# A list scheduler with narrow matmuls kept together, a second modulation group on TensorE, and softmax scaling on GpSimd

## The chip, the cores and the metric

One Trainium2 chip; the kernel runs on one of its cores. The metric is device microseconds of the execution. The kernel before takes 1565.89 us, the median of three runs (1565.12 to 1569.17).

## What is computed

A network of three layers in fp32 on 256 tokens of width 1024. Layer 0 works on two streams, the tokens x and a context ctx of 256 rows; layer 1 uses the context for keys and values only; the second block has tokens alone. What the change touches is the modulation and the softmax of the first two layers:

```python
ml = (silu(c) @ w_mod[i] + b_mod[i]).reshape(B, 6, 1, D)      # i = 0, 1
mc = (silu(c_ctx) @ w_mod[i] + b_mod[i]).reshape(6, D)
hl = rms_norm(xl) * (1 + ml[:, 1]) + ml[:, 0]                 # and hc from mc
oc, ol = mla_pool_mixer(hc, hl, ...)  if i == 0  else  gqa_mixer(...)
xl = xl + ml[:, 2] * ol
xl = xl + ml[:, 5] * conv_ffn(rms_norm(xl) * (1 + ml[:, 4]) + ml[:, 3], ...)
# layer 0: the same for xc with mc
s = einsum('bqhgd,bkhd->bhgqk', q, k) * scale
p = softmax(s)                                                # 8 heads in either mixer
o = einsum('bhgqk,bkhd->bqhgd', p, v)
```

Layer 0's mixer is latent attention (8 heads, queries of x on 512 keys, queries of ctx on 256) beside a pooling branch (cumulated means over windows of 2, 4, 8 and 16); layer 1's is grouped-query attention on 512 keys. The second block has a swiglu FFN, differential and dilated attention, gates, and another swiglu FFN.

## The kernel before

**Products.** Every weight arrives as a piece of up to 1 MB in one of three `raw` buffers. ScalarE (ACT) copies it to fp32r, `whi`; VectorE (DVE) subtracts that from the piece and has the rest, `wlo`. Activations are split the same way, and `mm3` makes of each product three fp32r matmuls (hi hi, hi lo, lo hi), `mm2` two.

**Order.** Nothing is issued as it is written. `Program` records each operation with its engine, its dependences and a priority (its index in the program, with a shift that a few places set). `schedule` then simulates the engines: it gives each operation the duration that `price` returns, takes on each engine the ready operation that is first by priority, hands out the slots of the pools (34 activations, 3 raw, 7 tmp, 24 small, 8 PSUM banks and so on), and sorts by simulated start. What comes out is each engine's program, which the chip runs in that order, whatever the real durations are. So `price`, the latencies and the DMA rate decide only the order. Each recorded operation is issued from one line, L401 in the profile of before.

**Modulation.** `silu(c) @ w_mod` has only two rows (token and context), so it is not done as other products. Pieces 0 and 1 of layer 0, which the first norm needs, come in eight chunks (`mod_chunk`): 16 fp32 matmuls of 32 columns by 128 each, four column groups of the PE array side by side (`mod<-wm,sc`), then a matmul with `sel`. The other pieces are six groups, `MODS` (`mod_group`), in eight steps k:

- group 0 (piece 2, both streams; in `WHOLE`) is done on TensorE: at each k four narrow fp32 matmuls, one per column group, 512 columns each (`mod<-raw,sc`). They are recorded at the end of each head of layer 0's attention (`fill`).
- groups 1 to 5 are done on DVE: at each k the weights are multiplied by one number per partition and added to an accumulator `macc` of 128x1024, once for each stream (a TENSOR_SCALAR at k = 0, a SCALAR_TENSOR_TENSOR at the seven others); at the end, narrow matmuls with a column of ones sum over the partitions (`mod<-macc,one`). Group 1 (piece 4, both streams) is recorded beside the products `uk`, `uv` and `uq` of the attention's start (`early`); groups 2 to 5 beside layer 0's FFN.

**Start.** 100 matmuls of a constant tile (`warm`) are recorded in `setup` with a shift that lets real work pass them. While they run, the first chunks of modulation and weights arrive.

**Layer 0's mixer.** Products `cq`, `ckv` and `p` per stream; GpSimd (POOL) makes running sums of p (`pp`); the raw products are copied from PSUM (`cqraw`), transposed on TensorE (`cT`) and scaled; then the attention.

**Softmax** (`softmax_t`): DVE takes the row's negative maximum from PSUM, ACT makes the exponentials with their sum, DVE the reciprocal, and `times` scales the tile of exponentials `e`: in layer 0 on DVE for x (16 tiles of 128x512) and on ACT for ctx (16 of 128x256), in layer 1 on ACT (16 of 128x512). TensorE then transposes two scaled tiles into one bank (`pt`); the result is split and multiplied by v (`o`).

**FFN.** `modnorm` makes `h`, the normed and modulated input of layer 0's FFN, for both streams: a column sum, POOL's power -1/2, a spread over rows on TensorE (`rows`), and for each of 8 pieces two DVE and two ACT operations. `layer0_ffn` then starts the products `g` and `u`.

Of the kernel before, what the change touches and what calls it, by code (L numbers as in the profile page):

```python
# [29 lines left out]
WHOLE = (0,)  # L30
# [125 lines left out]
class Op:  # L156
    __slots__ = ("engine", "method", "args", "kw", "prio", "deps", "users", "n", "ready", "cost", "roots", "new",
                 "start", "end", "index", "outs")
# [10 lines left out]
class Program:  # L169
# [3 lines left out]
    TO_TENSOR = 110.0  # L173
    TABLES = {AF.Exp: 1, AF.Silu: 2, AF.Sin: 2, AF.Sigmoid: 3}
# [3 lines left out]
    DMA_RATE = 330.0  # L178
# [17 lines left out]
    def record(self, engine, method, args, kw):  # L196
        op = Op()
        op.engine, op.method, op.args, op.kw = engine, method, args, kw
        op.index = len(self.ops)
# [18 lines left out]
        for v in outs:  # L218
            g = self.region(v)
            r = v.root  # L220
            if r.cls == "psum" and engine == "tensor":
                if r.lastpe is not None:
                    op.deps.add(r.lastpe)
                r.lastpe = op.index
            for o, q in r.writes + r.reads:
                if o != op.index and self.overlap(g, q):
                    op.deps.add(o)
            cover = lambda q: g[0] <= q[0] and q[1] <= g[1] and g[2] <= q[2] and q[3] <= g[3] and \
# [16 lines left out]
    def price(op):  # L245
# [5 lines left out]
        if op.engine == "tensor":  # L251
            if m == "transpose":
                return 109.0 * n / 128
            width = out.parts[1] - out.parts[0]
            if op.kw["lhsT"].root.dtype == F32R:
                return n / 2.4 * (1 if n >= 256 else 4) + 2.5
            c = max(128, n) * 4 / 2.4 + 2.5
            return c * 0.25 + 15 if width == 32 else c
        if op.engine == "scalar":
            src = op.args[1]  # L260
            extra = sum(93 for k in ("scale", "bias") if isinstance(op.kw.get(k), View))
            return (0.833 * n + (52 if src.root.cls == "psum" else 93) + extra
                    + (60 if op.kw.get("accum_out") is not None else 0))
# [9 lines left out]
        if op.engine == "gpsimd":  # L273
            if op.kw.get("op") == ALU.pow:
                return 300 + 165.0 * n
            return 100 + n * {"tensor_tensor": 2.3, "tensor_scalar": 1.46, "memset": 0.8}.get(m, 3.5)
        return 60.0

# [4 lines left out]
    def schedule(self, capacity):  # L283
# [21 lines left out]
        dma, heat, table = 0.0, {}, None  # L305
# [6 lines left out]
        while len(order) < N:  # L312
            best = None
            for e in self.ENGINES:
                if avail[e]:
# [13 lines left out]
            _, i = heapq.heappop(avail[e])  # L329
# [17 lines left out]
            for r in need:  # L347
                free[r.cls].sort()
                r.slot = free[r.cls].pop(0)[1]
                live[r.cls][front:r.first] += 1  # L350
            op.start = t
            cost = op.cost
# [10 lines left out]
            if e == "sync":  # L363
                begin = max(t, dma)
                dma = begin + self.nbytes(op) / self.DMA_RATE
                op.end = dma + self.DMA_LATENCY
# [38 lines left out]
class Net:  # L405
# [159 lines left out]
    def setup(self):  # L565
# [19 lines left out]
        for _ in range(100):  # L585
            nc.tensor.matmul(ps[:, :T], lhsT=warm[:, :P], rhs=warm, start=True, stop=True)
# [41 lines left out]
    def mod_chunk(self, k):  # L628
        nc = self.nc
        ps = self.ps("mod")  # L630
        for i in range(KD // 2):
            for q in range(4):
# [3 lines left out]
                                 start=(i == 0), stop=(i == KD // 2 - 1))  # L636
        sb = self.tmp(P, "modsb")
# [5 lines left out]
    def mod_group(self, g):  # L643
# [6 lines left out]
        for k in range(KD):  # L650
            r = self.raw(f"wmod{g + 1}", k, 4 * w)
            if g in WHOLE:
                ps = ps or self.ps("mod")
                for q in range(4):
                    nc.tensor.matmul(ps[32 * q:32 * q + 32, :w], lhsT=self.sc[:, k, :], rhs=r[:, q * w:(q + 1) * w],
                                     start=(k == 0), stop=(k == KD - 1))
            else:
# [11 lines left out]
        ps = ps or self.ps("mod")  # L669
        for s in range(streams if acc else 0):  # L670
            for q in range(4):
                h, o = divmod(q * w, D)
                nc.tensor.matmul(ps[32 * q:32 * q + 32, :w], lhsT=self.one[:, s], rhs=acc[h, s][:, o:o + w],
                                 start=(s == 0), stop=(s == streams - 1))
        sb = self.tmp(w, "modsb")
# [56 lines left out]
    def times(self, engine, x, r):  # L732
# [3 lines left out]
        else:  # L736
            self.nc.vector.tensor_scalar(x, x, r, None, op0=ALU.mult)
# [40 lines left out]
    def layer0_mixer(self):  # L778
# [194 lines left out]
        for hd in range(8):  # L973
# [13 lines left out]
            for s in range(2):  # L987
                k0, nk = (0, 4) if s == 0 else (T, 2)
                es = []
                for j in range(2):  # L990
# [4 lines left out]
                    es.append(self.softmax_t(pscore[:, :nk * P], nk * P, "scalar" if s else "vector"))  # L995
# [66 lines left out]
    def layer0_ffn(self, acc):  # L1062
# [3 lines left out]
        acc2 = [self.acc(s) for s in range(2)]  # L1066
        fill = self.mod_groups(range(2, len(MODS)))
# [70 lines left out]
    def layer1(self, acc):  # L1138
# [27 lines left out]
        for b in range(4):  # L1166
# [13 lines left out]
            for hd in range(2):  # L1180
                kv = (b * 2 + hd) // 4
                es = []
                for j in range(2):
# [3 lines left out]
                    es.append(self.softmax_t(pscore, 512, "scalar"))  # L1187
# [695 lines left out]
```

## Time and profile before

| | before |
|---|---|
| median of three runs | 1565.89 us (1565.12 to 1569.17) |
| the profiled execution | 1562.85 us |
| its span, first to last instruction | 1561.1 us |
| mean granted TensorE clock | 0.997 |
| busy: PE, PEld, DVE, ACT, POOL | 98%, 86%, 74%, 53%, 6% |
| DMA | 258.47 MB, mean 166 GB/s |

The span is what the trace covers; the execution's time is 1.75 us longer. PE is the matmul engine and PEld its weight load, which runs beside it. A matmul's record can be longer than what it adds to the stream, because matmuls are pipelined; what one adds is read from the next one's start, or from the chain of waits. An fp32 matmul leaves two records, so four narrow matmuls are "x8" there.

### The profile page before, as it was taken

The page shows a single profiled execution, that of the slowest core. Times are in us where ns is not written, and L with a number is a line of the kernel's source. Part 1 is how long each engine was busy: PE and PEld are TensorE (multiplying, and loading weights), DVE is VectorE, ACT ScalarE, POOL GpSimd, SP SyncE. Part 2 cuts the span into 40 slices and gives each one's busy share as a digit, 9 for nine tenths or more (in the row PEclk, how much of TensorE's full clock was granted, in tenths as well). Part 3 has the DMA queues.
Part 4 walks back from the last instruction along what each step waited for, and adds up shares of the span by engine and source line. Part 5 has one row for each costly group of instructions (what it writes and reads, how often), then busy time and mean ns, then how long its engine had stood idle before and what let it go on. Part 6 is the DMA issues. An engine that isn't in the chain of part 4 may idle for free.

```text
span 1561.1 us, 23690 instructions
## 1 busy us (share of the span) xinstructions
PE 1534.3 (98%) x9226; PEld 1340.2 (86%) x9226; DVE 1147.6 (74%) x2117; ACT 829.1 (53%) x1532; POOL 100.1 (6%) x116
## 2 busy tenths in 40 slices
PE   9989999999999999999999999999999999999998
PEld 7877798888788888999888888888999999888886
DVE  5598889648964856889987787765887786687752
ACT  5356844231331334686876675554765565475550
POOL 0040000000000000110000011100000000111100
PEclk9999999999999999999999999999999999999999
DMA  9345353334753642222665564455423345454450
GB/s 373 117 133 215 135 177 133 123 109 180 257 185 133 245 155 86 84 107 109 237 221 192 177 227 162 163 206 197 166 87 114 122 168 200 173 216 162 162 189 27
DMA packets 41375, 258.47 MB, mean 166 GB/s; under 512 B 4784, under 2 KB 5168, under 8 KB 15664
## 3 DMA queue, kind: packets, MB, share of 16 engines
q1 hardware_dynamic: 41264, 256.97, 45.9%
q8 instruction: 72, 1.18, 0.3%
q14 instruction: 39, 0.32, 0.1%
HBM read 255.90 MB, written 1.05 MB: 165 GB/s over the span
## 4 chain that ended last, share of the span: by engine, by line
PE 88%; DVE 4%; ACT 1%; issue 1%; POOL 1%; DMA 0%; DVEq 0%; POOLq 0%; ACTq 0%; SPq 0%
PE g L401 18%; PE u L401 18%; PE dn L401 12%; PE tm L401 10%; PE y L401 8%; PE out L401 4%; PE gate L401 3%; PE s L401 3%; PE o L401 3%; PE pt L401 2%; PE pa L401 1%; PE mod L401 1%; PE uq L401 1%; DVE wlo L401 1%; DVE h L401 1%
## 5 line engine op out<-in xcount | busy, mean ns | idle before, releaser
L401 DVE TENSOR_TENSOR wlo<-raw,whi 128x1024 fp32r<-128x1024 f32 (+4 forms) x393 | 460.3, 1185 | 81.7 <-PE y L401 26.8
L401 ACT ACTIVATE whi<-raw 128x1024 fp32r<-128x1024 f32 (+4 forms) x393 | 394.1, 1025 | 221.5 <-PE dn L401 59.8
L401 PE MATMUL dn<-mid,whi 128*128 128x512 f32 (+1 forms) x576 | 172.2, 373 | 0.0
L401 PE MATMUL g<-h,whi 128*128 128x512 f32 (+1 forms) x528 | 169.7, 388 | 0.9 <-ACT h L401 0.8
L401 PE MATMUL u<-h,whi 128*128 128x512 f32 (+1 forms) x528 | 167.9, 385 | 0.0
L401 PE MATMUL tm<-whi,a 128*128 128x256 f32 (+1 forms) x576 | 126.8, 306 | 0.1
L401 PEld LDWEIGHTS dn<-mid,whi 128*128 128x128 f32 x576 | 105.0, 188 | 20.4 <-issue 0.8
L401 PE MATMUL dn<-mid,wlo 128*128 128x256 f32 (+1 forms) x376 | 121.6, 323 | 0.0
L401 PE MATMUL g<-a,whi 128*128 128x512 f32 x336 | 118.9, 392 | 0.0
L401 PE MATMUL u<-a,whi 128*128 128x512 f32 x336 | 118.7, 392 | 0.0
L401 PEld LDWEIGHTS g<-h,whi 128*128 128x128 f32 x528 | 99.2, 190 | 22.6 <-ACT h L401 0.9
L401 PEld LDWEIGHTS u<-h,whi 128*128 128x128 f32 x528 | 98.8, 188 | 19.8
L401 PE MATMUL g<-h,wlo 128*128 128x256 f32 (+1 forms) x344 | 115.0, 335 | 0.4 <-DVE wlo L401 0.4
L401 PE MATMUL u<-h,wlo 128*128 128x256 f32 (+1 forms) x344 | 114.6, 333 | 0.0
L401 PE MATMUL y<-whi,mid 128*128 128x512 f32 x352 | 109.0, 389 | 0.0
L401 DVE SCALAR_TENSOR_TENSOR macc<-raw,sc,macc 128x1024 f32<-128x1024 f32 x84 | 107.0, 1298 | 2.6 <-DMA raw<-wmod 2.4
L401 PEld LDWEIGHTS tm<-whi,a 128*128 128x128 f32 x576 | 95.2, 190 | 1.4 <-DVE a L401 0.3
L401 PE MATMUL g<-a,wlo 128*128 128x256 f32 x336 | 94.2, 280 | 0.0
L401 PE MATMUL u<-a,wlo 128*128 128x256 f32 x336 | 94.1, 280 | 0.0
L401 POOL TENSOR_TENSOR small<-small,mhalf 128x2 f32<-128x2 f32 (+2 forms) x34 | 34.2, 1007 | 895.1 <-DVE small L401 725.3
L401 PE MATMUL tm<-wlo,a 128*128 128x256 f32 (+1 forms) x288 | 87.6, 305 | 0.0
L401 PEld LDWEIGHTS y<-whi,mid 128*128 128x128 f32 x352 | 66.1, 188 | 13.7
(342 smaller groups left out, 3205.4 us busy)
## 6 DMA issues: line engine op xcount, KB each, us to landing
raw<-wup SPq DMA_DIRECT2D x44, 1024.0 KB, 4.8
raw<-wgu SPq DMA_DIRECT2D x44, 1024.0 KB, 4.8
raw<-wmod SPq DMA_DIRECT2D x32, 1024.0 KB, 5.0
raw<-wd SPq DMA_DIRECT2D x20, 1024.0 KB, 4.7
raw<-wdn SPq DMA_DIRECT2D x16, 1024.0 KB, 4.8
raw<-win2a SPq DMA_DIRECT2D x12, 1024.0 KB, 4.8
raw<-win2d SPq DMA_DIRECT2D x12, 768.0 KB, 4.2
wm<-wmod SPq DMA_DIRECT2D x16, 512.0 KB, 10.6
```

Source lines behind the costliest of these rows:

```text
L401: getattr(getattr(nc, op.engine), op.method)(*[res(a) for a in op.args], **{k: res(v) for k, v in op.kw.items()})
```

## The change

- `WHOLE` is now (0, 1): group 1 is done on TensorE as group 0 is, with four narrow matmuls of 256 columns at each k (32 in all). Its 16 `macc` operations and four of its narrow matmuls per stream are gone.
- `together` ties the narrow matmuls of one chunk, one k or one group: the first inherits the dependences of all, and `schedule` issues them back to back.
- Scheduler: a PSUM tile counts as one region in the dependences; entering and leaving narrow matmuls costs 90 and 230 ns in the model; a weight load sets a least distance of 109 ns between matmuls; DVE and POOL exclude each other in the model where `shared` says so; the DMA rate is 400 instead of 330, with a beginning of 2 us and at most 8 transfers ahead; other prices.
- 50 `warm` matmuls instead of 100.
- All 48 scalings of `e` in the two mixers go to POOL, as tensor_scalar.
- The first `macc` operation of group 2 waits in the model for the end of layer 0's `modnorm` (`late`).

The diff, cut to its core:

```diff
-WHOLE = (0,)
+WHOLE = (0, 1)
...
-    DMA_RATE = 330.0
+    DMA_RATE = 400.0
+    DMA_BEGIN = 2000.0
+
+    DMA_DEPTH = 8
...
+    def together(self, i):
+
+        group = self.ops[i:]
+        for op in group[1:]:
+            group[0].deps |= {d for d in op.deps if d < i}
+        for a, b in zip(group, group[1:]):
+            a.next = b
...
     def region(v):
+        if v.root.cls == "psum":
+            return (0, P, 0, v.root.ix.size)
...
+            if self.shared(op):
+                other = "gpsimd" if e == "vector" else "vector"
+                t = max(t, port[other])
+                port[e] = t + cost
+            if e == "tensor":
+                load = self.load(op)
+                t = max(t, begun + load)
+                if narrow != (load == 0.0):
+                    t = max(t, clock[e] + (self.LEAVE if narrow else self.ENTER))
+                begun, narrow = t, load == 0.0
+                follow = op.next
...
-        for _ in range(100):
+        for _ in range(50):
             nc.tensor.matmul(ps[:, :T], lhsT=warm[:, :P], rhs=warm, start=True, stop=True)
...
             if g in WHOLE:
                 ps = ps or self.ps("mod")
+                first = len(nc.ops)
                 for q in range(4):
                     nc.tensor.matmul(ps[32 * q:32 * q + 32, :w], lhsT=self.sc[:, k, :], rhs=r[:, q * w:(q + 1) * w],
                                      start=(k == 0), stop=(k == KD - 1))
+                nc.together(first)
...
                             nc.vector.tensor_scalar(acc[h, s], x, c, None, op0=ALU.mult)
+                            if g == 2:
+                                nc.ops[-1].deps.add(self.late)
...
-            self.nc.vector.tensor_scalar(x, x, r, None, op0=ALU.mult)
+            getattr(self.nc, engine).tensor_scalar(x, x, r, None, op0=ALU.mult)
...
-                    es.append(self.softmax_t(pscore[:, :nk * P], nk * P, "scalar" if s else "vector"))
+                    es.append(self.softmax_t(pscore[:, :nk * P], nk * P, "gpsimd"))
...
         acc2 = [self.acc(s) for s in range(2)]
+        self.late = len(self.nc.ops) - 1
         fill = self.mod_groups(range(2, len(MODS)))
...
-                    es.append(self.softmax_t(pscore, 512, "scalar"))
+                    es.append(self.softmax_t(pscore, 512, "gpsimd"))
```

What each engine issues: PE 8957 instructions before and 8931 now, DVE 2119 and 2087, ACT 1394 and 1362, POOL 121 and 169, the DMA queue 289 both times.

**Three places in the order.** In a row, a tile's name comes with its number in the program, and "x4" is four such instructions in a row. First, PE in layer 0's attention, before: `mod` are the narrow matmuls of group 0, `s` scores, `o` products with v, `pt` transposes of `e`.

```order
L401 MATMUL o_1733<-pT_1720,v_1236 64x256
L401 MATMUL mod_1533<-raw_1591,sc 32x512
L401 MATMUL s_1737<-qkT_1358,qkT_1639 128x512
...
L401 MATMUL pt_1832<-ident,e_1790 128x128
L401 MATMUL mod_1533<-raw_1591,sc 32x512
L401 MATMUL pt_1836<-ident,e_1790 128x128
L401 MATMUL mod_1533<-raw_1591,sc 32x512
L401 MATMUL s_1842<-qkT_1367,qkT_1692 128x256 x3
```

and with the change:

```order
L459 MATMUL s_1735<-qkT_1579,qkT_1572 128x512 x3
L459 MATMUL mod_1473<-raw_1519,sc 32x512 x4
L459 MATMUL o_1760<-pT_1723,v_1138 64x256 x3
...
L459 MATMUL s_2001<-qkT_1929,qkT_1924 128x256
L459 MATMUL mod_1473<-raw_1581,sc 32x512 x4
L459 MATMUL qkT_2039<-ident,qk_1132 96x128
```

Before, the 32 matmuls of group 0 stand at 15 places of PE's order; now they stand at 8, four at each. The chunks of `mod_chunk` (128 matmuls) stood at 15 places and stand at 8. The 32 new matmuls of group 1 stand at 8 places among `uk`, `uv` and `uq`.

Second, DVE at the copy of `cq` out of PSUM (`cqraw`), for which PE's transposes `cT` wait; `df` and `d` belong to the pooling branch. Before:

```order
L401 TENSOR_SCALAR macc_1054<-raw_785,sc 128x1024
L401 SCALAR_TENSOR_TENSOR df_1060<-pp_183_1025,pp_110 128x512
L401 TENSOR_TENSOR wlo_1067<-raw_594,whi_1040 128x1024
L401 TENSOR_TENSOR d_1072<-df_1060,d_1072 128x512
L401 TENSOR_SCALAR macc_1090<-raw_785,sc 128x1024
L401 SCALAR_TENSOR_TENSOR macc_1054<-raw_1019,sc,macc_1054 128x1024
L401 SCALAR_TENSOR_TENSOR macc_1090<-raw_1019,sc,macc_1090 128x1024
L401 COPY cqraw_1126<-cq_942 128x384
```

and with the change:

```order
L459 SCALAR_TENSOR_TENSOR df_963<-pp_179_932,pp_86 128x512
L459 TENSOR_TENSOR wlo_971<-raw_593,whi_944 128x1024
L459 TENSOR_TENSOR d_974<-df_963,d_974 128x512
L459 TENSOR_TENSOR wlo_1012<-raw_593,whi_995 128x1024
L459 TENSOR_TENSOR pp_183_1022<-pp_183_1022,consts 128x2
L459 COPY cqraw_1049<-cq_883 128x384
```

The four `macc` operations ahead of the copy are gone, and a second `wlo` stands there.

Third, DVE at the entry of layer 0's FFN, where POOL waits for `small` (the column sum of the second stream). Before:

```order
L401 SCALAR_TENSOR_TENSOR h_2963<-X_84,mods,rows_2903 128x256
L401 SCALAR_TENSOR_TENSOR h_2967<-X_84,mods,rows_2903 128x256
L401 TENSOR_SCALAR small_2973<-sum_2910 128x2
L401 SCALAR_TENSOR_TENSOR macc_2540<-raw_2877,sc,macc_2540 128x1024
L401 SCALAR_TENSOR_TENSOR h_2970<-h_2963,mods,h_2970 128x256
```

and with the change:

```order
L459 SCALAR_TENSOR_TENSOR h_2891<-X_84,mods,rows_2827 128x256
L459 TENSOR_SCALAR small_2898<-sum_2834 128x2
L459 RECIPROCAL sig<-lamL 128x1
L459 TENSOR_SCALAR ovs<-lamL 128x1
L459 TENSOR_TENSOR siglam<-sig,lam 128x1
L459 SCALAR_TENSOR_TENSOR h_2894<-h_2886,mods,h_2894 128x256
```

The `macc` of group 2 behind `small` is gone from here; its first one stands behind the last `h` of the second stream. Some operations of one column, for the second block, stand here instead.

## Rows read from the trace of the kernel before

**Rows 1.** The page: busy us and share of each engine; shares of the chain that ended last.

```profile
PE 1534.3 (98%) x9226; PEld 1340.2 (86%) x9226; DVE 1147.6 (74%) x2117; ACT 829.1 (53%) x1532; POOL 100.1 (6%) x116
...
PE 88%; DVE 4%; ACT 1%; issue 1%; POOL 1%; DMA 0%; DVEq 0%; POOLq 0%; ACTq 0%; SPq 0%
```

**Rows 2.** Windows: stretch, length, busy us (instructions) of engines, PEclk, DMA share, GB/s.

```profile
20.00:40.00 20.00, 19.46 (x200) 14.79 (x199) 13.40 (x29) 9.93 (x20) 0.71 (x1) 1.00 1.03 410
...
93.58:96.99 3.41, 3.24 (x13) 2.85 (x14) 3.34 (x17) 1.16 (x4) 2.39 (x3) 0.50 0.49 173
...
243.77:247.18 3.41, 3.41 (x18) 3.41 (x17) 3.41 (x11) 1.67 (x4) 0.00 (x0) 0.50 0.00 0
```

**Rows 3.** PE's waits over the span: us in total, times, longest us.

```profile
PE cT L401 <- DVE cqraw L401: 4.8, 1, 4.8
```

**Rows 4.** Timeline, 82 to 97 us (start us, us, engine, operation; idle before in brackets).

```profile
85.22 6.92 POOL L401 TENSOR_TENSOR pp<-pp 128x542 f32<-128x542 f32 x4 [1.29 <-DVE df L401]
...
89.12 4.11 DVE L401 SCALAR_TENSOR_TENSOR macc<-raw,sc,macc 128x1024 f32<-128x1024 f32 x2
93.15 0.55 DVE L401 COPY cqraw<-cq 128x384 f32<-128x384 f32 x1
...
93.75 1.33 PE L401 MATMUL cT<-ident,cqraw 128*128 128x128 f32 x5 [4.77 <-DVE cqraw L401]
```

**Rows 5.** The chain of waits, 120 to 180 us: start us, us, what.

```profile
125.00 0.62 PE mod L401 x8
...
128.12 1.06 PE mod L401 x8
...
133.50 0.99 PE mod L401 x8
...
142.58 0.97 PE mod L401 x2
...
178.32 0.98 PE mod L401 x4
```

**Rows 6.** By tile (macc, pp): count, duration ns min/median/max, first and last start, forms.

```profile
L401 DVE SCALAR_TENSOR_TENSOR macc<-raw,sc,macc x84: 1273/1278/2099, 89.1 to 551.1; 128x1024 f32<-128x1024 f32 x84
L401 DVE TENSOR_SCALAR macc<-raw,sc x12: 742/746/1580, 82.9 to 509.1; 128x1024 f32<-128x1024 f32 x12
L401 POOL TENSOR_TENSOR pp<-pp x10: 1091/1524/2118, 75.4 to 96.0; 128x542 f32<-128x542 f32 x4, 128x538 f32<-128x538 f32 x3, 128x530 f32<-128x530 f32 x2, 128x514 f32<-128x514 f32 x1
L401 POOL MEMSET pp<- x4: 547/552/699, 0.8 to 2.4; 128x544 f32 x4
```

**Rows 7.** Timeline of PE at the start.

```profile
17.16 3.28 PE L401 MATMUL warm<-warm 128*128 128x256 f32 x26
...
28.59 0.41 PE L401 MATMUL mod<-wm,sc 128*32 128x128 f32 x2
28.93 0.50 PE L401 MATMUL p<-h,wlo 128*128 128x512 f32 x1
```

**Rows 8.** Timeline at the entry of the first FFN.

```profile
247.10 1.27 DVE L401 SCALAR_TENSOR_TENSOR macc<-raw,sc,macc 128x1024 f32<-128x1024 f32 x1
...
247.26 1.67 POOL L401 TENSOR_TENSOR small<-small,mhalf 128x2 f32<-128x2 f32 x1 [6.55 <-DVE small L401]
...
248.99 0.71 PE L401 MATMUL rows<-ident,small 128*128 128x128 f32 x4 [0.64 <-POOL small L401]
```

**Rows 9.** POOL by tile small (columns as in Rows 6).

```profile
L401 POOL TENSOR_TENSOR small<-small,mhalf x34: 550/734/1674, 10.7 to 1555.8; 128x2 f32<-128x2 f32 x24, 128x1 f32<-128x1 f32 x6, 128x4 f32<-128x4 f32 x4
```

**Rows 10.** Groups by form: count, busy us, mean ns, idle before.

```profile
L401 DVE TENSOR_SCALAR e<-e,small 128x512 f32<-128x512 f32 x16 | 7.7, 479 | 0.2
L401 ACT ACTIVATE e<-e,small 128x512 f32<-128x512 f32 x16 | 10.8, 727 | 0.0
L401 DVE TENSOR_TENSOR wlo<-raw,whi 128x1024 fp32r<-128x1024 f32 x348 | 421.7, 1224 | 77.4 <-PE y L401 26.8 <-PE dn L401 18.2 <-ACT whi L401 12.9
```

**Rows 11.** Windows of the second layer's mixer (columns as in Rows 2).

```profile
sum 98.00, PE 97.11 PEld 92.09 DVE 84.88 ACT 70.79 POOL 13.70; mean PE 13.87 PEld 13.16 DVE 12.13 ACT 10.11 POOL 1.96
```

More of the change, by code (lines that the diff above doesn't have):

```diff
@@ L157 @@
     __slots__ = ("engine", "method", "args", "kw", "prio", "deps", "users", "n", "ready", "cost", "roots", "new",
-                 "start", "end", "index", "outs")
+                 "start", "end", "index", "outs", "next")
 class Engine:
@@ L198, in record @@
         op.engine, op.method, op.args, op.kw = engine, method, args, kw
+        op.next = None
         op.index = len(self.ops)
@@ L252, in price @@
             if m == "transpose":
-                return 109.0 * n / 128
-            width = out.parts[1] - out.parts[0]
+                return 55.0
             if op.kw["lhsT"].root.dtype == F32R:
-                return n / 2.4 * (1 if n >= 256 else 4) + 2.5
-            c = max(128, n) * 4 / 2.4 + 2.5
-            return c * 0.25 + 15 if width == 32 else c
+                return n / 2.4 + 13.3
+            return 0.4 * n if out.parts[1] - out.parts[0] == 32 else 222.0
         if op.engine == "scalar":
@@ L261, in price @@
             extra = sum(93 for k in ("scale", "bias") if isinstance(op.kw.get(k), View))
-            return (0.833 * n + (52 if src.root.cls == "psum" else 93) + extra
-                    + (60 if op.kw.get("accum_out") is not None else 0))
+            return (0.833 * n + (52 if src.root.cls == "psum" else 110) + extra
+                    + (92 if op.kw.get("accum_out") is not None else 0))
         if op.engine == "vector":
@@ L274, in price, with load, shared @@
             if op.kw.get("op") == ALU.pow:
-                return 300 + 165.0 * n
+                return 700.0
             return 100 + n * {"tensor_tensor": 2.3, "tensor_scalar": 1.46, "memset": 0.8}.get(m, 3.5)
         return 60.0
+    @staticmethod
+    def load(op):
+        if op.method != "transpose" and op.outs[0].parts[1] - op.outs[0].parts[0] == 32:
+            return 0.0
+        return 109.0
+    @staticmethod
+    def shared(op):
+        big = [v for v in list(op.args) + list(op.kw.values()) if isinstance(v, View)
+               and v.root.cls != "psum" and not any(v is o for o in op.outs)]
+        if op.engine == "gpsimd":
+            return len(big) > 0
+        if op.engine != "vector":
+            return False
+        big = [v for v in big if v.ix.size > 1]
+        return len(big) > 1 or (op.method in ("tensor_copy", "tensor_scalar") and len(big) == 1
+                                and op.outs[0].root.cls != "psum")
     def nbytes(self, op):
@@ L304, in schedule @@
         clock = {e: 0.0 for e in self.ENGINES}
-        dma, heat, table = 0.0, {}, None
+        dma, heat, table = self.DMA_BEGIN, {}, None
+        port = {"vector": 0.0, "gpsimd": 0.0}
+        begun, narrow, follow = 0.0, False, None
+        landed = []
         done = np.zeros(N + 1, bool)
@@ L314, in schedule @@
             for e in self.ENGINES:
-                if avail[e]:
+                if e == "tensor" and follow is not None:
+                    t = clock[e]
+                elif avail[e]:
                     t = clock[e]
@@ L328, in schedule @@
                 heapq.heappush(avail[e], (p, i))
-            _, i = heapq.heappop(avail[e])
+            if e == "tensor" and follow is not None:
+                i = follow.index
+                avail[e].remove((follow.prio, i))
+                heapq.heapify(avail[e])
+            else:
+                _, i = heapq.heappop(avail[e])
             op = ops[i]
@@ L350, in schedule @@
                 live[r.cls][front:r.first] += 1
+            cost = op.cost
+            if self.shared(op):
[9 more added lines that the diff above has]
+                follow = op.next
             op.start = t
[L352 removed]
             if e == "tensor":
@@ L363, in schedule @@
             if e == "sync":
+                landed.append(op)
+                if len(landed) > self.DMA_DEPTH:
+                    t = max(t, landed[-1 - self.DMA_DEPTH].end)
+                    op.start, clock[e] = t, t + cost
                 begin = max(t, dma)
@@ L653, in mod_group @@
                 ps = ps or self.ps("mod")
+                first = len(nc.ops)
                 for q in range(4):
@@ L656, in mod_group @@
                                      start=(k == 0), stop=(k == KD - 1))
+                nc.together(first)
             else:
@@ L669, in mod_group @@
         ps = ps or self.ps("mod")
+        first = len(nc.ops)
         for s in range(streams if acc else 0):
@@ L674, in mod_group @@
                                  start=(s == 0), stop=(s == streams - 1))
+        if acc:
+            nc.together(first)
         sb = self.tmp(w, "modsb")
```

3 lines of the change are left out of this document (2 added, 1 removed).

## The prediction

> **What bounds the kernel now.** I read the page first: PE is busy for 98% of the span and holds 88% of the chain that ended last [rows 1]. So the end moves only by what PE's own stream loses or gains; DVE, ACT and POOL count where PE waits for them. Next I looked for the places where PE issues less than it could: the windows, PE's list of waits, the timeline, the chain. They show four kinds. (a) PE stands once for 4.77 us, for the copy of `cq` out of PSUM [rows 3, 4]; right behind it the granted clock is 0.50, that is 1.2 instead of 2.4 GHz, from 93.58 to 96.99 us [rows 2]. A second stretch of that kind follows the waits at the FFN's entry, 243.77 to 247.18 us [rows 2]. (b) In layer 0's attention the chain is all PE, and pieces of it are the narrow matmuls `mod`. A burst of four of group 0 (x8) holds the chain for 0.99 us, a burst of a single matmul (x2) for 0.97 [rows 5]: the burst is paid, not the matmul. There are 15 of them, from the first at 128.12 us to the one that follows the last row shown. (c) The start, where DMA moves 410 GB/s [rows 2] and PE fills time with `warm`. (d) Small waits for norms, as at 248.99 us [rows 8].
>
> The sum goes against the profiled execution, 1562.85 us (span 1561.1). The median of the runs shown is 1565.89, 3.0 us higher; I take the difference off that median.
>
> **The change, part by part.**
>
> 1. Group 0 in whole bursts. 15 places become 8: 7 fewer at 0.97 to 0.99 us [rows 5] = **-6.8**. Nothing covers them, since PE is the chain there. As one matmul and four cost the same, the other end is small: if leaving and entering were cheaper next to work that waits anyway, -6.0.
>
> 2. The wait for `cqraw`. Ahead of that copy DVE runs four `macc` operations of group 1; the last two alone take from 89.12 to 93.15 us, and POOL's running sums run beside them [rows 4]. They go. What is left ahead is `wlo`, one more than before, at 1.22 us [rows 10]. PE's wait of 4.77 and the slow stretch behind it (3.24 us busy at half clock [rows 2], so 1.6 too much) are 6.4 together. I leave 1.0 for a DVE that is still in a `wlo` when `cq` ends: **-5.4**. Ends: -6.4 (no wait), and -3.5 (two `wlo` late, 2.4 us, and some of the slow stretch).
>
> 3. Group 1 on TensorE. Its two final bursts of 32x256 go and eight of the same shape come, 0.62 us each [rows 5]: 6 x 0.62 = **+3.7**. All of it is on the path, since PE is full there. Upper end, at the price of a 512-wide burst: 8 x 0.97 - 1.2 = +6.5. DVE loses 14 x 1.28 + 2 x 0.75 = 19.4 us of work [rows 6]; beyond step 2 I count that at nothing, because the chain of the attention that follows is all PE, whose one wait for DVE of this kind is that of step 2 [rows 3]. The `raw` buffers of group 1 are now let go by PE, whose bursts stand early enough that no later load is held longer; nothing.
>
> 4. The start. `mod_chunk` goes from 15 places to 8. A single narrow matmul at 28.59 us moves the next `p` by 0.34 us [rows 7]; five of the seven lie behind 25 us, where PE is the bound: -1.7. The other side is `warm`: 26 of them fill 17.16 to 20.44 us [rows 7], and now the 50 are over before the first chunk has come. PE then stands for some 3 us at a time, which is what comes ahead of both slow stretches above. One such stretch of 3.41 us in work that is on the path costs 1.7; I take two thirds of one, +1.2. Together **-0.5**, ends -1.7 (none) and +3.4 - 1.7 = +1.7 (two), or more (rival C).
>
> 5. FFN entry. POOL's power for the second stream takes 1.67 us beside a `macc` of 1.27 [rows 8], where the median of these is 0.73 [rows 9]; PE waits 0.64 for it. With the `macc` held back that wait goes: **-0.6**. Ends -0.9 (the whole excess) and +0.5 (the small operations that stand there now).
>
> 6. Scaling on POOL: 32 tiles in layer 0, 16 in layer 1. No row shows POOL's tensor_scalar. Below it lies a memset of nearly the same tile, 0.55 us, which reads nothing; above it the addition of two tiles, 1.09 to 2.12 us [rows 6]. I take 0.8, nearer the first, since it reads one tile. DVE took 0.48 and ACT 0.73 [rows 10]. So a pair of tiles reaches `pt` at most some 0.6 us later, and in layer 0 PE has other heads' scores, bursts and products to issue meanwhile: 0. DVE and ACT get 7.7 and 10.8 us back (and ACT those of the narrower tiles), which PE does not wait for: 0. In layer 1 DVE's `wlo` runs beside POOL, and the rows show what that does: beside POOL's running sums two `macc` take 4.11 us, and at most 2.10 instead of 1.28 or 1.58 instead of 0.75 each [rows 4, 6], so 0.8 us more. 16 meetings make 13 us of DVE time; DVE has 98 - 84.9 = 13.1 us idle there [rows 11]. I take **+2**, because a good part fits in idle time; ends 0 and +8. The Trainium skill, Perfetto Trace Analysis, section "Optimizing Scalar/DVE Operations", says that GpSimd and DVE share a read port, "so offloading operations between those two might not help". The trace agrees as far as those longer `macc` go; by this rule the step would be rival A.
>
> 7. Everything else that the new prices reorder: **0**, ends -3 and +3; outside the places above PE's stream has next to no gaps to win.
>
> Sum: -6.8 - 5.4 + 3.7 - 0.5 - 0.6 + 2 = **-7.6**. The profiled execution would come to 1555.2, the median to **1558.3 us**.
>
> **The rivals.**
>
> A. *POOL takes from DVE what DVE needs.* In layer 1 all 16 scalings meet a `wlo`; 13 us of lost DVE time against 13.1 idle, and the idle time isn't where it is wanted. PE then waits for `wlo` for some 7 us: about 1565, no change. For it: DVE at 87% of that stretch [rows 11]. Against it: `wlo` is prepared ahead as far as three raw buffers go, and PE shows hardly a wait for it now. The Trainium skill, SBUF — State Buffer, section "Who interferes with whom", has a lock on that port held for whole instructions. The trace agrees: the increase of 0.8 us is a good part of one POOL addition [rows 6].
>
> B. *The other side, slower.* The scaling sits between exponential and `pt`, on every one of 24 pairs of tiles. If PE runs out of other work there, each pair adds its full delay: POOL's price above DVE's or ACT's, up to 0.3 us, and half a `wlo` of waiting for the port, twice per pair where both tiles queue: some 0.8 us, 24 x 0.8 = 19 us. That gives -7.6 + 19 = +11.4, 1577. It decides from the point where POOL's queue of two tiles (1.6 us, or 3 with waits) is longer than the products between a head's scores and its transposes. Against it: the scores of the next pair stand ahead of `pt` in PE's order.
>
> C. *The start at half clock.* With 50 `warm` matmuls gone PE may be at 0.50 for most of 12 to 28 us instead of one stretch: +8, some 1566.
>
> D. *The bursts don't pay.* If the 0.97 us belonged to the bank or the operands and not to the change between shapes, whole bursts would cost four times as much as the x2 rows; the x8 rows of 0.99 speak against it. It would give 1565.
>
> **How the numbers follow.** Forecast 0.66, A 0.14, B 0.09, C 0.07, D 0.04. A measurement of this kernel tells 0.3% (4.7 us) from no change: faster is below 1561.2, slower above 1570.6. Around the forecast the ends of the steps give 1550 (all good ends but the last) to 1562; A, C and D lie within 0.3% of before, B above. A small part of the forecast's own range is within 0.3% too (0.03), and of A and C some lies on the faster side (0.05). So faster 0.68, same 0.22, slower 0.10. The range runs from 1549.5 to 1568, which leaves out B and a little at the lower end.
>
> **What would show it.** In the profile after: `cT` waits 1 us or less and there is no slow stretch at 93 us; eight x8 pieces `mod` of 0.99 and eight of 0.62 in the chain before 200 us; macc x70 and x10; PE's wait for `rows` at the FFN's entry below 0.2; POOL's tensor_scalar near 0.8. Wrong would be: a clock of 0.50 before 30 us for more than one stretch (C); PE waiting for `wlo` in layer 1 (A) or for `e` (B); more than eight bursts or a price above 1.1 each (D).

## The result, and the profile after

The changed kernel takes 1578.46 us (median of four runs, 1574.98 to 1582.78) against 1565.56 for the kernel before in the same measurement: 1.0081 times, 95% interval 1.0061 to 1.0101. The forecast was 1558.3 us. The profiled execution is the one of 1578.47 us, its span 1576.7 us against 1561.1 before.

The lines of the page of the changed kernel that answer to [rows 1] and to `wlo` in [rows 10]:

```profile
PE 1537.3 (98%) x9224; PEld 1337.2 (85%) x9224; DVE 1123.4 (71%) x2085; ACT 816.0 (52%) x1500; POOL 170.3 (11%) x164
...
PE 83%; DVE 7%; ACT 3%; DMA 2%; POOL 2%; issue 2%; DVEq 0%; SPq 0%; POOLq 0%; ACTq 0%
...
L459 DVE TENSOR_TENSOR wlo<-raw,whi 128x1024 fp32r<-128x1024 f32 (+4 forms) x393 | 460.9, 1186 | 79.4 <-PE y L459 22.0
```

PE is as busy as before (3 us more), but the chain has 83% of it instead of 88%: the rest has gone to DVE, ACT, DMA and POOL. So PE's stream did not get longer by work; it got holes. PE's waits (us in total, times, longest) say which:

```profile
PE pt L459 <- POOL e L459: 13.1, 21, 1.5
PE cq L459 <- ACT h L459: 3.6, 1, 3.6
...
PE cT L459 <- ACT junk L459: 0.2, 1, 0.2
```

The wait for `cqraw` of [rows 3] is gone, as forecast. In its place stand 21 waits of the transposes `pt` for POOL's scaled `e`, 13.1 us together. POOL by form (busy us, mean ns, idle before), and the tile `e` (ns minimum, median, maximum):

```profile
L459 POOL TENSOR_SCALAR e<-e,small 128x512 f32<-128x512 f32 x32 | 55.5, 1744 | 71.7 <-DVE small L459 66.4 <-PE s L459 4.2 <-ACT e L459 1.0
...
L459 POOL TENSOR_SCALAR e<-e,small 128x256 f32<-128x256 f32 x16 | 15.6, 986 | 6.3 <-DVE small L459 6.3
```

```profile
L459 POOL TENSOR_SCALAR e<-e,small x48: 917/1562/2748, 128.1 to 711.8; 128x512 f32<-128x512 f32 x32, 128x256 f32<-128x256 f32 x16
```

The scaling that was estimated at 0.8 us takes 1.56 us for a 512-wide tile when nothing disturbs it (23 of the 32 take 1.56 to 1.58), 0.92 for a 256-wide one, and up to 2.75. One such place in layer 1, from the timeline:

```profile
691.14 7.38 POOL L459 TENSOR_SCALAR e<-e,small 128x512 f32<-128x512 f32 x4 [5.50 <-DVE small L459]
...
692.60 1.22 DVE L459 TENSOR_TENSOR wlo<-raw,whi 128x1024 fp32r<-128x1024 f32 x1
...
692.76 0.44 PE L459 MATMUL pt<-ident,e 128*128 128x128 f32 x2 [0.27 <-POOL e L459]
...
695.49 0.87 PE L459 MATMUL pt<-ident,e 128*128 128x128 f32 x6 [1.35 <-POOL e L459]
```

POOL works off four tiles in a row, 7.38 us. PE starts the pair's first two transposes at 692.76 us and the other six only at 695.49, because POOL's second tile began beside a `wlo` of DVE (692.60 to 693.82) and took 2.75 us. It was POOL that waited: `wlo` has its 1.22 us, and over all 348 pieces of 128x1024 DVE's mean is 1.228 us now and was 1.224.

Windows of the kernel before and then of the changed one (columns as in [rows 2]):

```profile
15.50:25.60 10.10, 9.71 (x119) 8.56 (x117) 6.63 (x16) 4.92 (x14) 0.71 (x1) 1.00 1.02 410
160.00:200.00 40.00, 39.94 (x249) 30.68 (x249) 34.56 (x75) 32.91 (x74) 0.00 (x0) 1.00 0.37 133
655.00:720.00 65.00, 64.66 (x446) 59.26 (x445) 56.33 (x129) 53.12 (x118) 6.09 (x5) 1.00 0.27 98
```

```profile
15.50:25.60 10.10, 7.27 (x76) 5.86 (x77) 5.15 (x13) 3.80 (x10) 0.70 (x1) 0.50 1.03 410
...
160.00:200.00 40.00, 35.35 (x221) 27.57 (x219) 27.90 (x61) 28.33 (x61) 22.80 (x16) 0.96 0.40 143
655.00:720.00 65.00, 58.53 (x393) 51.54 (x392) 49.12 (x111) 39.02 (x91) 32.29 (x21) 1.00 0.19 68
```

At the start the clock is at half for 10.1 us, where before it was at full; in the last 40 us of layer 0's attention PE has 35.35 us of work instead of 39.94 and one stretch at half clock; in layer 1's mixer (655 to 720 us) PE is busy for 58.53 of 65 us instead of 64.66.

Where the time went stands in a ledger of places in PE's stream, the starts or ends of operations in the two traces (us from the span's start):

```
place                                before    after   difference
first p                               25.12    28.90     +3.8
first transpose cT                    71.25    70.41     -0.8
first uk                              97.17    88.46     -8.7
last pt of layer 0                   198.14   200.80     +2.7
first g of layer 0's FFN             242.59   243.48     +0.9
first scores of layer 1              653.92   654.29     +0.4
last pt of layer 1                   705.93   715.82     +9.9
end of layer 1's FFN                 904.90   917.66    +12.8
first scores of the second block    1114.98  1128.79    +13.8
last pt of the second block         1275.07  1286.69    +11.6
last matmul                         1553.98  1569.93    +16.0
```

Up to the attention the change is ahead by 8.7 us. Layer 0's attention gives it all back (+11.4), layer 1's mixer loses 9.5, and layer 1's FFN, in which nothing was changed, 3.3 (of that below).

### The profile page after: what moved, and what is told of

Read it like the earlier page. It is cut to its first block, busy times and chain, and to the rows that moved or that the text cites. A ratio compares the mean times of both kernels' runs of the same rounds, so it can differ in the third digit from the quotient of the medians.

```text
span 1576.7 us, 23785 instructions
## 1 busy us (share of the span) xinstructions
PE 1537.3 (98%) x9224; PEld 1337.2 (85%) x9224; DVE 1123.4 (71%) x2085; ACT 816.0 (52%) x1500; POOL 170.3 (11%) x164
## 4 chain that ended last, share of the span: by engine, by line
PE 83%; DVE 7%; ACT 3%; DMA 2%; POOL 2%; issue 2%; DVEq 0%; SPq 0%; POOLq 0%; ACTq 0%
PE u L459 18%; PE g L459 18%; PE dn L459 10%; PE tm L459 8%; PE y L459 8%; PE gate L459 3%; PE out L459 3%; PE o L459 2%; DVE small L459 2%; POOL e L459 2%; DVE wlo L459 2%; PE mod L459 2%; PE p L459 1%; PE s L459 1%; PE pa L459 1%
## 5 line engine op out<-in xcount | busy, mean ns | idle before, releaser
L459 DVE SCALAR_TENSOR_TENSOR macc<-raw,sc,macc 128x1024 f32<-128x1024 f32 x70 | 87.9, 1280 | 9.9 <-DMA raw<-wmod 9.9
L459 POOL TENSOR_SCALAR e<-e,small 128x512 f32<-128x512 f32 (+1 forms) x48 | 70.9, 1491 | 78.0 <-DVE small L459 72.7
```

The costliest lines, as they stand in the source:

```text
L459: getattr(getattr(nc, op.engine), op.method)(*[res(a) for a in op.args], **{k: res(v) for k, v in op.kw.items()})
```

## The experiments

Two theories stood against each other at first, and the recorded expectations go by their letters. **S**: the scaling on POOL is too long a link between exponential and transposes. **O**: the new order is worse in itself. A third, **W**, was the start.

### The scaling back, and the scaling alone

```diff
-                    es.append(self.softmax_t(pscore[:, :nk * P], nk * P, "gpsimd"))
+                    es.append(self.softmax_t(pscore[:, :nk * P], nk * P, "scalar" if s else "vector"))
...
-                    es.append(self.softmax_t(pscore, 512, "gpsimd"))
+                    es.append(self.softmax_t(pscore, 512, "scalar"))
```

> The changed kernel with the softmax scaling where it was before (layer 0: DVE for x, ACT for ctx; layer 1: ACT), everything else as changed. Theory S (scaling): POOL's tensor_scalar takes 1.56 us for 128x512 and 0.92 for 128x256 and stands between exponential and transposes; it cost 9.5 us in layer 1's mixer and more than 10 in layer 0's attention. Then this takes 1552 to 1560 us and PE's waits of pt for e (13.1 us) are gone. Theory O (order): the scheduler's new rules made the loss; then 1573 to 1579, with other waits in place of those. Theory W (warm): the start at half clock made it; then also above 1570.

Measured: 1562.84 us, 0.9967 of the kernel before (0.9954 to 0.998), 2.8 us above the range of S and far from O and W. It is 15.6 us below the changed kernel by the medians, and 17.8 us when each is held against the kernel before in its own measurement. The waits for POOL are gone; 4.2 us of PE's waits are put down to ACT's `e`:

```profile
PE o L459 <- ACT e L459: 1.6, 1, 1.6
...
PE pt L459 <- ACT e L459: 1.2, 2, 0.9
...
PE s L459 <- ACT e L459: 0.7, 1, 0.7
PE out L459 <- ACT e L459: 0.7, 1, 0.7
```

So the attention isn't won back whole: from the first `uk` to the last `pt` of layer 0 this variant takes 104.5 us and the kernel before 101.0, and 3.3 us of these waits lie there. In the other direction, the kernel before with that edit reversed (and `times` calling the engine named, as in the change):

> The kernel before with all 48 scalings of the two mixers on POOL, nothing else. S: slower by 17 to 25 us, 1582 to 1590, with waits of pt for POOL's e in both mixers. O and W: within 5 us of before.

Measured: 1586.01 us, 1.0114 (1.0098 to 1.0129), 18.3 us above the kernel before. By the ledger its loss is 10.0 us up to the last `pt` of layer 0 and 8.7 more up to the last of layer 1. PE's waits:

```profile
PE pt L401 <- POOL e L401: 12.8, 19, 3.7
PE cT L401 <- DVE cqraw L401: 4.8, 1, 4.8
```

Both hold for S: the scaling is worth 16 to 18 us in either order. O and W are out as the main cause. The waits named are 12.8 us only; beside them stand two longer stretches at half clock (200.3 to 207 us, and the stretch at the FFN's entry twice as long). The longest wait, 3.7 us, belongs to a POOL tile that took 5.32 us: three `wlo` ran on DVE one after the other from 196.50 to 200.17 us, each in its usual 1.2 us, and POOL was done only behind them.

```profile
196.28 6.86 POOL L401 TENSOR_SCALAR e<-e,small 128x512 f32<-128x512 f32 x2 [6.77 <-DVE small L401]
...
201.65 0.69 PE L401 MATMUL pt<-ident,e 128*128 128x128 f32 x2 [3.72 <-POOL e L401]
```

### The start

```diff
-        for _ in range(50):
+        for _ in range(100):
```

> The changed kernel with 100 warm matmuls. W: the granted clock stays 1.00 from 5 us on, and the time falls by 8 us or more, since PE keeps its lead. S: the first p comes about 3.8 us earlier as before, but the attention's waits follow POOL, so the time falls by 0 to 4 us: 1574 to 1578.

Measured: 1578.78 us, 1.0069 (1.0048 to 1.0091): no difference from the changed kernel, 0.8 us above the range of S and without the 8 us of W. The window that was at half clock:

```profile
15.50:25.60 10.10, 9.82 (x120) 8.85 (x119) 6.33 (x15) 5.22 (x13) 0.71 (x1) 1.00 1.03 412
```

The clock is at full again, the first `p` comes 1.9 us earlier and layer 0's attention ends 2.9 us earlier. In layer 1 that lead is gone (first scores at +0.5 us against +0.4, last `pt` at +11.5 against +9.9); two stretches at half clock stand there now, at 617 and 696 us. W is out for this kernel; where the attention does not wait, see the last experiment.

### What the planner believes

`price` has POOL's tensor_scalar at 100 + 1.46 n ns, 847 for 512 columns, a line that the change leaves as it is. With 2.85 n it gives the measured 1.56 us for 512 columns, and 0.83 for 256, where 0.92 were measured:

```diff
-            return 100 + n * {"tensor_tensor": 2.3, "tensor_scalar": 1.46, "memset": 0.8}.get(m, 3.5)
+            return 100 + n * {"tensor_tensor": 2.3, "tensor_scalar": 2.85, "memset": 0.8}.get(m, 3.5)
```

> The changed kernel with the scheduler's price of POOL's tensor_scalar set from 0.85 to the 1.56 us that a 128x512 tile takes in the trace (2.85 ns per column instead of 1.46). If the loss is one of planning (S with a wrong price), a planner that knows it puts other work ahead of the transposes: 1566 to 1573. If the scaling's length is a loss that no order hides: 1575 to 1580.

Measured: 1573.89 us (1566.75 to 1576.37), 1.0032 (1.0017 to 1.0048), 4.6 below the changed kernel and between the two expectations, 0.9 above the first. PE's waits for POOL:

```profile
PE pt L459 <- POOL e L459: 2.7, 2, 2.4
```

In layer 0 PE no longer waits for it (both of these waits lie in layer 1): the last `pt` stands 9.1 us ahead of the kernel before, further than with the scalings back (4.9). In layer 1 it still costs: from the first scores to the last `pt` 8.0 us are lost. The window there has PE at 49.85 of 55 us and a granted clock of 0.94:

```profile
655.00:710.00 55.00, 49.85 (x323) 43.66 (x322) 41.30 (x92) 31.71 (x73) 27.52 (x19) 0.94 0.18 66
```

So the loss has two parts: in layer 0 a wrong price, in layer 1 a link that the right price alone does not hide. That PE has no other work there is the likely reason; no run tries another order of layer 1. Hence layer 0's scaling on POOL with the right price, layer 1's on ACT:

> The changed kernel with POOL's tensor_scalar priced at 1.56 us for a 512-wide tile, and layer 1's scaling back on ACT; layer 0's stays on POOL. With the right price the planner put other work ahead of layer 0's transposes (waits of pt for e: 2.7 us in the whole kernel), while layer 1 still lost 8 us between its first scores and its last transposes. Theory S (POOL's chain costs only where PE has nothing else, and the planner must know it): 1556 to 1563, below the variant with all scalings back. Rival O: if layer 0's gain in that variant was an accident of the order, 1563 to 1568.

Measured: 1559.29 us (1553.34 to 1564.95), 0.9955 (0.9937 to 0.9973). POOL's `e` is no longer among PE's twelve longest waits, and layer 0's last `pt` is 10.9 us ahead of before. By the time alone this variant is not told apart from the one with all scalings back (0.9967, 0.9954 to 0.998); what does tell them apart is the trace, 4.3 us less from the first `uk` to the last `pt` of layer 0. Does the right price alone do it, in the order of before? The kernel before, layer 0's scalings on POOL, priced right:

> The kernel before with layer 0's 32 scalings on POOL and POOL's tensor_scalar priced at 1.56 us. With the wrong price and both layers it lost 18 us, some 9 of them in layer 0. S: with the right price layer 0 loses nothing, 1561 to 1568, and PE's waits of pt for e are below 2 us there. If only the new rules of the scheduler can hide them: 1570 or more.

Measured: 1565.99 us, 0.9996 (0.9985 to 1.0007): no loss and no gain. Layer 0's last `pt` is 0.5 us behind the kernel before, where the wrong price had it 10 us behind. PE's wait:

```profile
PE pt L401 <- POOL e L401: 1.4, 3, 0.6
```

This holds for S once more: in layer 0 the price decides whether the scaling is hidden, not the other rules.

### The other steps

Ties between narrow matmuls, alone in the kernel before (in `together`, in `schedule`'s `follow`, and its calls in `mod_chunk` and `mod_group`; 8 places instead of 15 for either kind):

> The kernel before, with the narrow matmuls of one chunk or one k of group 0 tied together and nothing else (8 places instead of 15 for either). Prediction's step 1 and the gain of step 4: -6.8 and -1.7, so 1556 to 1559 against 1566, with first p, first cT and the end of layer 0's transposes earlier by that. Rival: the tied matmuls wait for the last one's data and give that back at the start or in the attention: within 3 us of before.

Measured: 1563.44 us, 0.9978 (0.9969 to 0.9987): 2.6 us, a third of what was expected, and within the 3 us of the rival. By the ledger the start gives 3.2 (first `cT`, where 1.7 were expected) and the attention another 2.7 (last `pt`, where 6.8 were expected); 2.2 are lost again up to layer 1's first scores, with a stretch at half clock at 612 us, and 3.1 in the last FFN (of that below). Three waits of PE are about what is missing in the attention, 3.7 us together; of them only the second stood in the list of before, with 0.2 us:

```profile
PE pt L419 <- ACT e L419: 1.7, 1, 1.7
...
PE uq L419 <- DVE wlo L419: 1.0, 2, 0.7
PE qkT L419 <- DVE qk L419: 1.0, 2, 0.5
```

And the ties taken out of the variant with the scalings back (`together` returns at once):

> The variant with all scalings back, and narrow matmuls not tied together (the scheduler may put others between them). Step 1 and 4: ties are worth 7 bursts of 0.97 and some of mod_chunk, so this is 6 to 9 us slower (1569 to 1572), unless the price of entering and leaving in the scheduler, which stays, keeps them together on its own: then equal within 2 us, with 8 places for each group in the trace.

Measured: 1569.23 us (1565.08 to 1575.96), 1.0019 (1.0006 to 1.0032), 6.4 above that variant. That fits the expected range, but not for the reason: its order still has group 0 at 11 places and `mod_chunk` at 15, its attention ends no later than the variant's (last `pt` 5.7 us ahead of before against 4.9), and what it loses it loses behind layer 1's mixer, in a stretch at half clock at 729 us and in the last FFN. This run does not show what the ties are worth.

Group 1 back on DVE, in the variant with the scalings back:

```diff
-WHOLE = (0, 1)
+WHOLE = (0,)
```

> The variant with all scalings back, and group 1 on DVE again (WHOLE is (0,)). Prediction's steps 2 and 3: group 1 on TensorE costs 8 bursts of 0.52 to 0.62 us less two, +3.7, but frees the copy of cq, -5.4. If so, this is 1 to 3 us slower than that variant (1564 to 1566), with PE's wait of cT for cqraw back at some 2 to 5 us. Rival: the new scheduler alone removes that wait; then this is 2 to 4 us faster (1559 to 1561).

Measured: 1576.76 us, 1.0066 (1.0043 to 1.0089), 13.9 above that variant by the medians and far outside both expectations. (The profiled execution is the fastest of four, 8.6 above that variant's; 7.8 of this stand at the last `pt` of layer 0.) The wait for `cqraw` does not come back: in the new order only one `macc` stands ahead of that copy. The other fifteen come behind it, from 104 us on, and delay what follows. PE's waits from 95 to 130 us:

```profile
PE uq L459 <- ACT whi L459: 3.1, 1, 3.1
PE po L459 <- DVE pool L459: 1.9, 1, 1.9
PE uq L459 <- DVE wlo L459: 1.9, 1, 1.9
PE qkT L459 <- DVE v L459: 1.9, 2, 1.2
```

and a window in the midst of them, at half clock while DVE is busy without a gap:

```profile
110.40:124.10 13.70, 8.34 (x24) 7.43 (x25) 13.70 (x19) 2.42 (x4) 0.00 (x0) 0.51 0.69 219
```

In this order group 1 on TensorE is the largest gain of the change: 8 bursts of 0.57 us buy DVE's time at the place where PE needs it. So the new order takes the wait for `cqraw` away by itself, and the move of group 1 pays behind it.

### A loss where nothing was changed

Layer 1's FFN took 185.2 us before (from the end of `out` to the end of `dn`) and 188.5 after. There PE alternates 512 columns (hi) and 256 (lo). A pair takes 346.7 ns before, in a pattern of 350 and 343, and 353.3 after, in a pattern of 350, 361, 349; the granted clock is 1.00 and DVE and ACT take their usual times. Each stage keeps one pattern from end to end. To see whether it is the alternation, two products are issued at once, hi, hi, lo, lo:

```diff
-        mm(out[:, T:2 * T], lhsT=l[1], rhs=r[:, 0], start=False, stop=stop)
+        lo = dict(out=out[:, T:2 * T], lhsT=l[1], rhs=r[:, 0], start=False, stop=stop)
+        held, self.held = getattr(self, "held", None), lo
+        if held is not None:
+            self.held = None
+            for x in (held, lo):
+                o = x.pop("out")
+                mm(o, **x)
```

> The same with the two-matmul products issued for two steps of k together: hi, hi, lo, lo (512, 512, 256, 256 columns) instead of hi, lo, hi, lo. In some FFN stages a pair hi, lo takes 353 ns (a pattern of 350, 361, 349) and in others 347 (350, 343), with the granted clock at 1.00 in both. If it is the alternation that falls into one of two patterns, all stages take 347 now and the time is 2 to 7 us below the run beside it; if the pattern has another cause, equal within 2 us.

Measured: 1560.17 us, 0.9961 (0.9948 to 0.9973), as the run beside it (1559.29). In its profile all stages have one value, 348.4 ns for each hi and lo, between the two. That speaks for the alternation as what falls into two patterns, by one profile, but the time says that the even order is no gain. Whether the pattern belongs to the program was tried by running the fastest variant again:

> The fastest variant so far once more, for its scatter (1553 to 1565 us) and a second profile. If the two patterns of hi and lo matmuls (347 and 353 ns a pair) belong to the program, the same stages show the same values as in its first profile (347 in layer 1's FFN and the second block's first FFN, 353 at the gates and in the last FFN); if they belong to the execution, they differ. Time within 4 us of 1559.

Measured: 1560.56 us, 0.996 (0.9949 to 0.9972). The second block's first FFN had 346.7 ns in the first profile and 353.3 in this one. The first and fifth hi of four pairs, in the first profile (1.39 us) and in the second (1.41):

```profile
980.05 0.39 PE L459 MATMUL u<-a,whi 128*128 128x512 f32 x1
...
981.44 0.39 PE L459 MATMUL g<-a,whi 128*128 128x512 f32 x1
```

```profile
979.90 0.40 PE L459 MATMUL u<-a,whi 128*128 128x512 f32 x1
...
981.31 0.40 PE L459 MATMUL g<-a,whi 128*128 128x512 f32 x1
```

So for this stage the pattern belongs to the execution: its 210 us are 2.3 us longer in the second profile. The other stages do not show that. The gates have 353 ns in the kernel before and in every variant that alternates, the last FFN the same value in both of these profiles. And layer 1's FFN has 353 in all three profiles with layer 1's scaling on POOL in the new order (the changed kernel, 100 `warm`, the right price) and 347 in all the others that alternate. So the 3.3 us lost there may hang on step 6; what sets the pattern stays open.

### The version that beats both

The priced variant with 100 `warm` matmuls:

> The fastest variant so far (POOL's scaling priced right and in layer 0 only) with 100 warm matmuls. In the changed kernel 100 of them made the first p 1.9 us earlier and took the stretch at half clock from 15 to 25 us away, but the waits that followed ate that. Where those are gone it should stay: 2 to 4 us below the run beside it. Rival: the start is bound by DMA and nothing is left by layer 0's FFN: equal within 2 us.

Measured: 1555.52 us (1553.28 to 1563.45), 0.9933 (0.9912 to 0.9953). That is 3.8 and 5.0 us below the two measurements of the variant with 50, whose intervals overlap with this one's. The mean clock of its profile is 0.997, against 0.995 and 0.992 of those two:

```profile
core 0: 1554.1 us, clock 0.997
```

## Why the prediction was wrong

The step that failed is **step 6**, "Scaling on POOL", +2 in the sum. Its price was 0.8 us and the traces show 1.56 (0.92 for the narrower tile): the estimate lay between a memset and an addition of two tiles and chose the memset's side, "since it reads one tile". POOL's scaling of one tile is longer than its undisturbed addition of two, 1.09 us for 542 columns [rows 6]; the number of operands was no guide. Its cover was "0" in layer 0, because PE "has other heads' scores, bursts and products to issue meanwhile". It has them (the runs with the right price show it), but the order is fixed ahead by a planner that believed 0.85 us, and the transposes stood where that put them. In layer 1 the price was sought in DVE's `wlo`; it kept its length there, and POOL waited. Measured for the whole step: +15.6 us between the changed kernel and the same with the scalings back (17.8 with each against its own kernel before).

**Rival B** is what happened: the scaling between exponential and `pt`, PE without other work there, 1577 us forecast and 1578.46 measured. It had 0.09. Its sum of 0.8 us a pair came out near (15.6 / 24 = 0.65), but partly by luck: it was put together from a POOL of 0.8 us instead of 1.56 and from half a `wlo` of waiting (0.6 us) for each tile, where the mean 512-wide tile lost 0.18 (1.74 against 1.56). Its argument against itself, that the scores of the next pair stand ahead of `pt`, depends on the planner's price of the operation, and that could have been read: it stands in `price`, next to lines that the change edits.

The other steps, with what the traces show:

- **Step 1**, -6.8: the price of a burst holds, 0.99 to 1.00 us for a whole one in the chain after (1.60 for one at half clock), at 8 places. Its worth does not: alone in the kernel before, the ties bring 2.7 us in the attention. "Nothing covers them, since PE is the chain there" was the fault; a chain that is all PE says that PE is last, not by how much. With the scalings back the stretch from the first `uk` to the last `pt` is 3.5 us longer than before, where steps 1 and 3 together made it 3.1 shorter.

```profile
91.62 0.57 PE mod L459 x8
...
117.68 0.57 PE mod L459 x8
...
123.82 1.00 PE mod L459 x8
...
131.26 0.99 PE mod L459 x8
...
171.35 1.60 PE mod L459 x8
```

- **Step 2**, -5.4: from the first `cT` to the first `uk` the kernel before takes 25.9 us and the changed one 18.1, -7.9. Wait and slow stretch are gone altogether. But that did not need group 1 to leave DVE: with group 1 on DVE in the new order these products take 16.6 us, without the wait.
- **Step 3**, +3.7: 0.57 us a burst, at most 0.64, as put (the first and the last of the eight in the rows above). But the 19.4 us of DVE work that were counted "at nothing" beyond step 2 were worth 13.9 in the order of the change, with the price of the bursts taken off already. And "no later load is held longer; nothing" left out that a burst itself waits for its piece, 1.1 us for `raw` from `wmod` in the changed kernel.
- **Step 4**, -0.5: -0.8 at the first `cT`. It consists of +3.8 up to the first `p`, with 10.1 us at half clock where two thirds of a stretch of 3.41 were counted, and -4.6 behind it. PE stood 3.6 us for ACT's `h` there, as put. The ties alone brought 3.2 at the first `cT` where 1.7 were counted, and 100 `warm` matmuls make it 2.0 earlier; so both terms were too small and nearly cancel. Rival C had the half clock right and its price, +8, wrong.
- **Step 5**, -0.6: POOL's second power takes 0.70 us instead of 1.67 [rows 8], and `rows` follows without a wait:

```profile
248.15 0.70 POOL L459 TENSOR_TENSOR small<-small,mhalf 128x2 f32<-128x2 f32 x1 [6.62 <-DVE sig L459]
...
249.48 0.60 PE L459 MATMUL rows<-ident,small 128*128 128x128 f32 x4
```

  From the first `g` to this `rows` the kernel before takes 6.40 us and the changed one 6.00, a gain of 0.4. No run has the `macc` held back alone.
- **Step 7**, 0: layer 1's FFN and the last FFN ran in the longer of two patterns, 3 to 4 us a stage against the profile of the kernel before. Whether that is the change's doing is not shown. The scheduler's other new rules were not run one by one either.
- **Rival A** did not come: `wlo` kept its length. The rule of the Trainium skill, Perfetto Trace Analysis, section "Optimizing Scalar/DVE Operations", that offloading between GpSimd and DVE might not help, was borne out in its result; the mechanism here was POOL's own length and its wait, at most 1.2 us a tile in the changed kernel (2.75 against 1.56), and not a slower DVE. **Rival D** did not come either.

Without step 6 the sum was -9.6, and the variant with the scalings back measured -4.9 (1562.84 against 1567.73): the direction right, the size half. The range was too narrow by its own terms, too: the upper ends of the seven steps add up to +10.2, which is 1576.1 us and not the 1562 or 1568 that the prediction gives, and the lower ends without step 7 to 1553.8 and not 1550. The measured 1578.46 lies above even that sum, because step 6 alone came to twice its upper end of +8.

## What to carry to other kernels

Where a planner's prices fix the order, an operation that moves to another engine runs by the order that its price made. Look up that price first and compare it with the longest similar row, since a wrong one turns a hidden link into a wait. Work taken off an engine that is busy for 98% of the span need not shorten the run by as much: what the engines that feed it can deliver at that place sets the gain. And do not count the time of a feeding engine as free because no wait for it shows yet: here taking work off DVE was the larger gain.

## What had not been expected of the hardware

- POOL's tensor_scalar with one number per partition: 0.92 us for 128x256, 1.56 for 128x512, that is 0.28 us and 2.5 ns a column, where its addition of two 542-wide tiles takes 1.09.
- Between POOL's scaling and DVE's two-input `wlo` only POOL waited: a tile took up to 2.75 us in the changed kernel, and 5.32 beside three `wlo` in a row in the kernel before with the scalings on POOL. `wlo` stayed at 1.2 us, even where it began in the midst of a POOL scaling (1.21 us at 661.91 us, 0.6 us into a tile). Beside POOL's two-input additions DVE's operations did get longer, [rows 6] and a `wlo` of the changed kernel that began in the midst of one:

```profile
77.21 1.09 POOL L459 TENSOR_TENSOR pp<-pp 128x542 f32<-128x542 f32 x1 [1.58 <-PE ckv L459]
77.30 2.08 DVE L459 TENSOR_TENSOR wlo<-raw,whi 128x1024 fp32r<-128x1024 f32 x1 [0.26 <-PE ckv L459]
```

- Alternating matmuls of 512 and 256 columns run a whole stage at 346.7 or at 353.3 ns a pair at the same granted clock, in one stage differently in two executions of one program.
- How long the clock is at half around waits of PE differs between executions of one program: at the start of one variant the profile shows it from 18.5 to 21.9 us, and in its second profile from 13.2 to 26.9.
